# Kept parts of activations, 132 seven-product pairs and shared taps in a two-layer fp32 trunk on one core

## The chip, the core and the metric

The kernel runs on one core of a Trainium2 chip. A core has a matrix engine (TensorE, PE in the profile; its weight loads are PEld), three engines for elementwise work (VectorE or DVE, ScalarE or ACT, GpSimd or POOL) and a queue engine (SyncE, SP) that issues DMA transfers between DRAM and the core's memory. Matmul results land in eight banks of 128 x 512 fp32, called PSUM; everything else lives in SBUF. The metric is the device time of one execution in microseconds, the median of three runs: 2468.08 us before the change (2467.96 to 2468.14).

## What is computed

Two layers over 256 frames of width 2048, all in fp32, batch 1. The first layer's mixer is a gMLP (u and v halves of 6144 each), the second's is latent attention (MLA). Behind each mixer stands a gated MLP with a causal convolution of width 3 over its up projection (2 x 5504 columns).

```python
def gmlp_mixer(x, w_in, ln_g, ln_b, w_s, b_s, w_out):
    z = jax.nn.gelu(x @ w_in)
    u, v = jnp.split(z, 2, axis=-1)
    v = layer_norm(v, ln_g, ln_b)
    ...
    s = jnp.einsum('gij,bnjgd->bnigd', w, v) + jnp.transpose(b_s)[None, None, :, :, None]
    return (u * s.reshape(B, S, GM_HALF)) @ w_out

def conv_ffn(x, w_up, conv_w, conv_b, w_down):
    h = x @ w_up
    h = lax.conv_general_dilated(h, conv_w[:, None, :], window_strides=(1,), padding=[(CONV_W - 1, 0)], ...) + conv_b
    a, g = jnp.split(h, 2, axis=-1)
    return (jax.nn.silu(g) * a) @ w_down

for i in range(DEPTH):        # DEPTH = 2: gMLP, then MLA
    x = layer_norm(ALPHA * x + mixer(x), ...)
    x = layer_norm(ALPHA * x + conv_ffn(x, ...), ...)
```

## The kernel before

**Products.** An fp32 product is built from three passes: each operand is split into a high part (the value rounded to the type fp32r, written by ScalarE) and a low part (the rest, written by VectorE), and TensorE computes high x high, high x low and low x high. The unit of work is a *step*: one weight tile of 128 x 2048, that is two slices k of the contraction by 1024 columns. SP loads it as `raw`, ScalarE casts it to `wh`, VectorE subtracts to `wl`. TensorE then runs 24 matmuls of 128 x 512 for the step (2 k, 2 halves of the frames, 2 halves of the columns, 3 passes).

**Seven-product pairs.** Some steps (116 in the kernel before) treat the pair of k and the halves as a 2 x 2 block product with seven products in place of eight, so 21 matmuls. They need sums of weight blocks, made by VectorE in `raw` in place (`raw<-raw`, one of 1024 columns and two of 512; `sum1`, `sum2`, lines 183 to 192), their high parts `th` on ScalarE and their low parts `tl` on VectorE (two each of 1024 columns; `high`, `rest`, lines 194 to 204). Only 1536 columns of `wh` and `wl` are then needed. They also need sums of activation blocks: `xs` for the projections from x, made once, and `wos`, `dn0s`, `dn1s` for the back projections, made when needed (`blocks`, line 740, and `sums1`, line 766: four instructions on 128 x 128, a cast and a low part on 512).

**Stages.** Steps are numbered over the whole program, and tiles carry the number (`raw184`, `wl126`): v half of the gMLP (0 to 47), u half (48 to 95), its back projection wo (96 to 143), the first up projection (144 to 233), the first down projection dn0 (234 to 277), the MLA, the second up projection, the second down projection dn1. v, u and up go in groups of eight steps that produce 1024 columns; `GROUP_V`, `GROUP_U` and `GROUP_UP` (lines 555 to 557) say which steps of a group are seven-product pairs and where they stand. Before, the ten groups of an up projection have 2, 2, 3, 2, 3, 2, 3, 2, 3, 2 of them.

**Back projections.** wo, dn0 and dn1 are run by the class `Down` (line 917) in two passes over the contraction, the first for 1024 columns and the second, in reverse order, for the other 1024. `SEVEN_WO` and `SEVEN_DN` (lines 558 and 559) list the k of the seven-product pairs of each pass. Before, each quad of four k is split into high and low parts (`woa0_4`, `dn0a0_3`, 128 x 2048: `split4`, line 719) in the first pass and, but for the last four pairs, again in the second (`woa1_4` and so on). The source of the split is the gated activation, which was parked in DRAM (`wosrc4`, `dn0src3`) and is fetched again for each pass (`pb4`, `ab0_3`).

**The convolution.** A group of an up projection is transposed into PSUM (`ht`), and for each tile of 128 columns x 256 frames ScalarE writes y = bias + w2 x, and VectorE adds the two shifted taps with one scalar_tensor_tensor each, of 255 and 254 columns (`taps`, line 1379). Four tiles (two of the a half, two of the g half) make a y of 128 x 4 x 256, from which silu and the gate follow.

**The order of the work.** The class `Plan` (line 292) keeps a list of jobs with an engine, an estimated cost, a due time and needs of buffers, simulates the engines' times and emits the jobs of each engine in the order it finds. `_due` (line 368) sets when the parts of a step are due ahead of its start, `_start` (line 418) when a job could begin, `_fits` whether its buffers are free. The buffers are 22 tiles of 128 x 2048 (`BIG`), `MID` = 3 and `T2` = 5 smaller ones, and the PSUM banks. Engines run their own list in order; DMA issues of SP go out in SP's order, and a DMA that waits holds back those behind it.

Of the kernel before, what the change touches and what calls it, by code (L numbers as in the profile page):

```python
# [563 lines left out]
def trunk(ctx: ExitStack, tc: tile.TileContext, x, xT, gm_in, gm_wout, ffn_up, ffn_dn,  # L564
# [352 lines left out]
    class Down:  # L917

        def __init__(self, n_k, gates, sevens, tag):
# [11 lines left out]
        def give(self, i, tile, after, again, view, stays=None):

            if stays is not None:
                self.here[0, i] = self.here[1, i] = stays, ()
                return
# [440 lines left out]
    def ffn(layer, ln, acc, end, last):  # L1376
        act = [None] * 6

        def taps(tiles, name):
# [33 lines left out]
        def tapped(tiles, name, t, bank, after=(), more=0):  # L1413

            a, m = tiles[0][0], len(tiles) // 2
            scale, add, silu, gate = taps(tiles, name)
            made = []
            for i in range(2 * m):
                due = plan.wide - 0.4 - 0.7 * (2 * m - 1 - i + 4 * more) if bank else t + 6 + i
                j = plan.job("A", maps(256), lambda i=i: scale(i), after if i == 0 else (j,), ready=t, due=due - 1.2,  # L1420
                             need={} if i else {"mid": 1})
                made.append(plan.job("V", adds(255, 2), lambda i=i: add(i), (j, *made[-1:]), ready=t, due=due,
                                     give={} if i < 2 * m - 1 else {"bank": 2} if bank else {"t2": 2}))
# [560 lines left out]
```

## Time and profile before

| | before |
|---|---|
| median of 3 runs | 2468.08 us (2467.96 to 2468.14) |
| the profiled execution, its own time | 2466.72 us |
| its span | 2464.9 us |
| mean granted TensorE clock | 0.998 |
| TensorE's weight loads (PEld) busy | 2053.0 us, 83% |
| DMA moved | 550.33 MB, mean 223 GB/s |
| of it read from / written to DRAM | 518.99 MB / 29.36 MB |
| instructions in the span | 30098 |

The span is the time from the first to the last instruction that the profile shows; the execution's own time is 1.8 us longer. Busy time of an engine is the sum of its instructions' times; the *chain that ended last* is found by going back from the last instruction, at each step to what released it. `PE wo L75 x24` in a timeline is 24 matmuls into tiles named wo, one after another; L75 is the line of a helper through which all instructions go, so that tiles tell more than lines. A group row of VectorE reads: output tile, input tiles, shape out<-in, count | busy us, mean ns of one | idle us ahead of them and what ended that idle time.

### The profile page before, as it was taken

The page shows a single profiled execution, that of the slowest core. Times are in us where ns is not written, and L with a number is a line of the kernel's source. Part 1 is how long each engine was busy: PE and PEld are TensorE (multiplying, and loading weights), DVE is VectorE, ACT ScalarE, POOL GpSimd, SP SyncE. Part 2 cuts the span into 40 slices and gives each one's busy share as a digit, 9 for nine tenths or more (in the row PEclk, how much of TensorE's full clock was granted, in tenths as well). Part 3 has the DMA queues.
Part 4 walks back from the last instruction along what each step waited for, and adds up shares of the span by engine and source line. Part 5 has one row for each costly group of instructions (what it writes and reads, how often), then busy time and mean ns, then how long its engine had stood idle before and what let it go on. Part 6 is the DMA issues. An engine that isn't in the chain of part 4 may idle for free.

```text
span 2464.9 us, 30098 instructions
## 1 busy us (share of the span) xinstructions
PE 2449.7 (99%) x11585; PEld 2053.0 (83%) x11585; DVE 2218.2 (90%) x2459; ACT 1375.1 (56%) x1388; POOL 1.9 (0%) x11
## 2 busy tenths in 40 slices
PE   9999999999999999999999999999999999999998
PEld 7888888888888888888888888988888888888886
DVE  7999899999998899999999897757799999999897
ACT  6555656656554555555566554555465555566562
POOL 0000000000000000000000000000000000000000
PEclk9999999999999999999999999999999999999999
DMA  8566666666676555646567775435556556477774
GB/s 341 207 231 223 217 217 226 239 239 242 236 256 255 206 187 202 232 163 242 202 252 265 267 259 213 169 137 214 185 201 221 187 207 232 163 248 260 272 247 166
DMA packets 127583, 550.33 MB, mean 223 GB/s; under 512 B 14160, under 2 KB 14544, under 8 KB 105808
## 3 DMA queue, kind: packets, MB, share of 16 engines
q1 hardware_dynamic: 126432, 541.99, 61.4%
q10 hardware_dynamic: 1008, 6.42, 0.6%
q8 instruction: 91, 1.49, 0.2%
q14 instruction: 52, 0.43, 0.0%
HBM read 518.99 MB, written 29.36 MB: 222 GB/s over the span
## 4 chain that ended last, share of the span: by engine, by line
PE 99%; DVE 1%; DMA 0%; issue 0%; ACT 0%; DVEq 0%
PE up L75 29%; PE dn L75 15%; PE wo L75 9%; PE v L75 9%; PE u L75 8%; PE up_p L75 5%; PE mo L75 4%; PE dn_p L75 2%; PE u_p L75 2%; PE upf L75 2%; PE v_p L75 2%; PE wo_p L75 1%; PE ht L75 1%; PE mkv L75 1%; PE kn L75 1%; PE qn L75 1%
## 5 line engine op out<-in xcount | busy, mean ns | idle before, releaser
L75 DVE TENSOR_TENSOR wl<-raw,wh 128x2048 fp32r<-128x2048 f32 (+3 forms) x456 | 935.3, 2077 | 51.6 <-ACT wh L75 42.1
L75 ACT CAST wh<-raw 128x2048 fp32r<-128x2048 f32 (+3 forms) x456 | 788.1, 1742 | 260.0 <-DMA raw<-in_ffn_up_dram 86.3
L75 PE MATMUL up<-wh,xhl 128*128 128x512 f32 x1888 | 522.1, 391 | 0.0
L75 ACT CAST th<-raw 128x1024 fp32r<-128x1024 f32 x232 | 244.1, 1053 | 378.8 <-DVE raw L75 376.9
L75 PEld LDWEIGHTS up<-wh,xhl 128*128 128x128 f32 x1888 | 353.2, 188 | 72.0
L75 DVE TENSOR_TENSOR raw<-raw 128x1024 f32<-128x1024 f32 x348 | 302.0, 868 | 9.0
L75 PE MATMUL up<-wl,xhl 128*128 128x512 f32 x944 | 295.0, 390 | 0.0
L75 DVE TENSOR_TENSOR tl<-raw,th 128x1024 fp32r<-128x1024 f32 x232 | 281.3, 1220 | 0.2 <-ACT th L75 0.2
L75 PEld LDWEIGHTS up<-wl,xhl 128*128 128x128 f32 x944 | 177.3, 188 | 36.9
L75 PE MATMUL wo<-wh,woa 128*128 128x512 f32 x586 | 162.8, 390 | 0.0
L75 DVE SCALAR_TENSOR_TENSOR y<-ht,cst,y 128x255 f32<-128x255 f32 x320 | 147.5, 479 | 13.0 <-ACT y L75 7.2
L75 PE MATMUL v<-wh,xhl 128*128 128x512 f32 x558 | 154.0, 391 | 1.6 <-ACT wh L75 1.6
L75 PE MATMUL dn<-wh,dn0a 128*128 128x512 f32 x534 | 147.9, 390 | 0.0
L75 PE MATMUL dn<-wh,dn1a 128*128 128x512 f32 x534 | 147.6, 390 | 0.0
L75 PE MATMUL u<-wh,xhl 128*128 128x512 f32 x516 | 145.2, 391 | 0.0
L75 ACT ACTIVATE y<-ht,cst 128x256 f32<-128x256 f32 x160 | 78.0, 574 | 94.7 <-PE ht L75 94.7
L75 PEld LDWEIGHTS wo<-wh,woa 128*128 128x128 f32 x586 | 109.9, 188 | 22.6
L75 PEld LDWEIGHTS v<-wh,xhl 128*128 128x128 f32 x558 | 104.8, 188 | 24.7 <-ACT wh L75 2.8
L75 PEld LDWEIGHTS dn<-wh,dn1a 128*128 128x128 f32 x534 | 100.2, 188 | 20.8
L75 PEld LDWEIGHTS dn<-wh,dn0a 128*128 128x128 f32 x534 | 100.2, 188 | 20.7
L75 PEld LDWEIGHTS u<-wh,xhl 128*128 128x128 f32 x516 | 96.2, 188 | 19.4
L75 PE MATMUL up_p<-th,xs 128*128 128x512 f32 x288 | 96.6, 389 | 0.0
(503 smaller groups left out, 3734.7 us busy)
## 6 DMA issues: line engine op xcount, KB each, us to landing
raw<-in_ffn_up_dram SPq DMA_DIRECT2D x320, 512.0 KB, 5.0
raw<-in_ffn_dn_dram SPq DMA_DIRECT2D x172, 512.0 KB, 5.8
raw<-in_gm_in_dram SPq DMA_DIRECT2D x99, 512.0 KB, 4.9
raw<-in_gm_wout_dram SPq DMA_DIRECT2D x96, 512.0 KB, 5.3
raw<-in_gm_in_dram SPq DMA_DIRECT2D x46, 1024.0 KB, 6.1
raw<-in_ml_out_dram SPq DMA_DIRECT2D x16, 1024.0 KB, 5.0
raw<-in_ml_b_dram SPq DMA_DIRECT2D x14, 1024.0 KB, 5.8
raw<-in_ffn_up_dram SPq DMA_DIRECT2D x12, 1024.0 KB, 4.8
```

Source lines behind the costliest of these rows:

```text
L75: r = f(*args, **kw)
```

## The change

Four things change together.

1. Seven-product pairs: 132 in place of 116. One more in v, three more in wo's second pass, two more in the second pass of each dn, four more in each up (now 2, 3, 3, 3, 3, 3, 3, 3, 3, 2). Their places in the groups and lists change as well.
2. Back projections: in the first pass, those split quads that the second pass needs again (ten for wo, nine for each dn), and the activation sums of the k that are seven-product pairs in both passes (five each), are written to DRAM by SP (`keep_copy`). The second pass fetches these instead of fetching the source and splitting it again. Sums that only the second pass needs are made from the fetched parts: one more addition of 512 columns (high + low) stands ahead of the four block instructions.
3. The taps: ScalarE writes, beside y, a second map e = w1 x of each tile. VectorE adds the tap of shift 2 per tile as before (254 columns), and the tap of shift 1 for four tiles in one addition of 4 x 255 columns.
4. Planner: `MID` 4 and `T2` 4; a cost function `fused` for scalar_tensor_tensor; and `_start` no longer counts the ends of what a load waits for (the load that precedes it).

```diff
-MID = 3
-T2 = 5
+MID = 4
+T2 = 4
...
+def fused(n, k=1):
+    return k * (0.125 + 0.00106 * n)
...
     def _start(self, j):
-        t = max([self.now[j.eng], j.ready] + [a.end for a in j.after])
+        t = max([self.now[j.eng], j.ready] + [a.end for a in j.after if j.kind != "load"])
...
+    def keep_copy(self, src, dst, lo, due, cost):
+
+        return self.job("S", cost, lambda: self.feed.sq.dma_start(dst, src), (lo,), due=due)
...
-SEVEN_WO = ((8, 14, 20, 26, 30, 34, 40), (40, 34, 28, 22, 16, 12))
-SEVEN_DN = ((8, 14, 18, 22, 26, 32), (34, 28, 22, 16, 12))
+SEVEN_WO = ((14, 20, 24, 26, 30, 34, 40), (42, 40, 38, 34, 30, 26, 22, 20, 12))
+SEVEN_DN = ((8, 14, 18, 22, 26, 32), (36, 32, 28, 26, 22, 18, 14))
...
     def sums1(src8, k, name, after, due, done):
...
+        half = done is None
+        if half:
+            x = tp.tile([P, 2, S], F32, tag="t2", name=f"{name}x", bufs=T2)
 
         def first():
+            if half:
+                hl = src8[0][:, k % 4 : k % 4 + 2].bitcast(F32)
+                ve.tensor_tensor(x, hl[:, :, 0:S], hl[:, :, S : 2 * S], ALU.add)
+            kk = x if half else src8[:, k % 8 // 2]
             blocks(kk[:, 0, :], kk[:, 1, :], [t[:, i, :] for i in range(4)])
...
         def need(self, k, half, due):
             q = k // 4
+            if q not in self.hl and half == 1:
+                t = slot([P, 4, 512], f"{self.tag}a1_{q}", F32R)
+                src, job = self.copies[q]
+                self.hl[q] = t, plan.fetch(src, t.bitcast(F32), (job,), due)
             if q not in self.hl:
...
+                if q in self.again:
+                    t, lo = self.hl[q]
+                    dst = dram.tile([P, 4, 512], F32, name=f"{self.tag}hl{q}")
+                    self.copies[q] = dst, plan.keep_copy(t.bitcast(F32), dst, lo, due + 4.0, 2.9)
             if k in self.sevens[half] and k not in self.sums:
+                if half == 1 and k in self.twice:
+                    r = tp.tile([P, 2, 512], F32R, tag="mid", name=f"{self.tag}s1_{k}", bufs=MID)
+                    src, job = self.copies["s", k]
+                    self.sums[k] = r, plan.job("S", 1.5, lambda: feed.sq.dma_start(r.bitcast(F32), src), (job,),
+                                               due=due - 7.0, need={"mid": 1})
+                    return
+                if half == 1:
+                    self.sums[k] = sums1(self.hl[q], k, f"{self.tag}s1_{k}", {self.hl[q][1]}, due, None)
+                    return
...
+                if k in self.twice:
+                    r, lo = self.sums[k]
+                    dst = dram.tile([P, 2, 512], F32, name=f"{self.tag}sum{k}")
+                    self.copies["s", k] = dst, plan.keep_copy(r.bitcast(F32), dst, lo, due + 4.0, 1.5)
...
             y = tp.tile([P, 4, S], F32, tag="mid", name=f"y{name}", bufs=MID)
+            e = tp.tile([P, 4, S], F32, tag="mid", name=f"e{name}", bufs=MID)
...
                 ac.activation(y[:, i], src, AF.Identity, bias=w(F, 3), scale=w(F, 2))
-
-            def add(i):
+                ac.activation(e[:, i], src, AF.Copy, scale=w(F, 1))
+
+            def tap(i):
                 F, src = tiles[i]
-                for d in (1, 2):
-                    ve.scalar_tensor_tensor(y[:, i, d:S], src[:, 0 : S - d], w(F, 2 - d), y[:, i, d:S], ALU.mult, ALU.add)
...
+                ve.scalar_tensor_tensor(y[:, i, 2:S], src[:, 0 : S - 2], w(F, 0), y[:, i, 2:S], ALU.mult, ALU.add)
+
+            def add():
+                ve.tensor_tensor(y[:, 0:n, 1:S], y[:, 0:n, 1:S], e[:, 0:n, 0 : S - 1], ALU.add)
```

The planner then places everything anew. Three places show it. The first is VectorE's list in the fifth group of the first up projection, before the change. There the taps of the fourth group are due (transposed tiles `ht0_3`; `y0_14` and `y0_16` are the convolution's outputs, four tiles each), and `raw184` holds the weights of the fifth group's first seven-product pair.

```order
L75 TENSOR_TENSOR wl184_7448<-raw184_7415,wh184_7447 128x1536
L75 SCALAR_TENSOR_TENSOR y0_14_7464<-ht0_3_0_0_7454,cst_176,y0_14_7464 128x255
L75 SCALAR_TENSOR_TENSOR y0_14_7464<-ht0_3_0_0_7454,cst_176,y0_14_7464 128x254
L75 SCALAR_TENSOR_TENSOR y0_14_7464<-ht0_3_0_0_7454,cst_176,y0_14_7464 128x255
L75 SCALAR_TENSOR_TENSOR y0_14_7464<-ht0_3_0_0_7454,cst_176,y0_14_7464 128x254
L75 TENSOR_TENSOR raw184_7415<-raw184_7415 128x2x512
L75 SCALAR_TENSOR_TENSOR y0_14_7464<-ht0_3_0_1_7455,cst_176,y0_14_7464 128x255
L75 SCALAR_TENSOR_TENSOR y0_14_7464<-ht0_3_0_1_7455,cst_176,y0_14_7464 128x254
L75 SCALAR_TENSOR_TENSOR y0_14_7464<-ht0_3_0_1_7455,cst_176,y0_14_7464 128x255
L75 SCALAR_TENSOR_TENSOR y0_14_7464<-ht0_3_0_1_7455,cst_176,y0_14_7464 128x254
L75 SCALAR_TENSOR_TENSOR y0_16_7478<-ht0_3_1_0_7468,cst_176,y0_16_7478 128x255
L75 SCALAR_TENSOR_TENSOR y0_16_7478<-ht0_3_1_0_7468,cst_176,y0_16_7478 128x254
```

The same place after the change; `e0_14` is ScalarE's second map.

```order
L75 TENSOR_TENSOR wl184_7512<-raw184_7438,wh184_7511 128x1536
L75 SCALAR_TENSOR_TENSOR y0_14_7526<-ht0_3_0_0_7516,cst_176,y0_14_7526 128x254 x2
L75 SCALAR_TENSOR_TENSOR y0_14_7526<-ht0_3_0_1_7517,cst_176,y0_14_7526 128x254
L75 TENSOR_TENSOR raw184_7438<-raw184_7438 128x2x512
L75 SCALAR_TENSOR_TENSOR y0_14_7526<-ht0_3_0_1_7517,cst_176,y0_14_7526 128x254
L75 SCALAR_TENSOR_TENSOR y0_16_7540<-ht0_3_1_0_7530,cst_176,y0_16_7540 128x254
L75 TENSOR_TENSOR y0_14_7526<-y0_14_7526,e0_14_7527 128x4x255
L75 SCALAR_TENSOR_TENSOR y0_16_7540<-ht0_3_1_0_7530,cst_176,y0_16_7540 128x254
L75 TENSOR_TENSOR raw184_7438<-raw184_7438 128x512 x2
L75 SCALAR_TENSOR_TENSOR y0_16_7540<-ht0_3_1_1_7531,cst_176,y0_16_7540 128x254
```

Of each tile, one instruction is left, the four-tile addition of 4 x 255 columns stands behind the last, and ahead of the first weight sum of `raw184` stand three tap instructions where four stood.

The second place is SP's list in the first pass of dn0, before: loads of weights (`raw`), and among them the fetches of the parked sources (`ab0_3`).

```order
L75 DMA raw238_9725<-in_ffn_dn_dram 128x1024 x2
L75 DMA ab0_2_9753<-dn0src2_8132 128x2048
L75 DMA raw239_9766<-in_ffn_dn_dram 128x1024 x2
L75 DMA raw240_9803<-in_ffn_dn_dram 128x1024 x2
L75 DMA raw241_9848<-in_ffn_dn_dram 128x1024 x2
L75 DMA raw242_9877<-in_ffn_dn_dram 128x1024 x2
L75 DMA ab0_3_9910<-dn0src3_8798 128x2048
L75 DMA raw243_9926<-in_ffn_dn_dram 128x1024 x2
L75 DMA raw244_9960<-in_ffn_dn_dram 128x1024 x2
L75 DMA raw245_9999<-in_ffn_dn_dram 128x1024 x2
L75 DMA raw246_10036<-in_ffn_dn_dram 128x1024 x2
L75 DMA ab0_4_10064<-dn0src4_9472 128x2048
```

The same stretch after; `dn0hl3` is the DRAM copy of the split quad `dn0a0_3`, `dn0sum14` that of the sums of k = 14.

```order
L75 DMA raw239_9879<-in_ffn_dn_dram 128x1024 x2
L75 DMA dn0hl3_9783<-dn0a0_3_9782 128x2048
L75 DMA raw240_9920<-in_ffn_dn_dram 128x1024 x2
L75 DMA dn0sum14_9828<-dn0s0_14_9827 128x1024
L75 DMA raw241_9963<-in_ffn_dn_dram 128x1024 x2
L75 DMA dn0hl4_9874<-dn0a0_4_9873 128x2048
L75 DMA raw242_10001<-in_ffn_dn_dram 128x1024 x2
L75 DMA ab0_3_10030<-dn0src3_8889 128x2048
L75 DMA dn0sum18_9909<-dn0s0_18_9908 128x1024
L75 DMA raw243_10074<-in_ffn_dn_dram 128x1024 x2
L75 DMA dn0hl5_9953<-dn0a0_5_9952 128x2048
L75 DMA raw244_10118<-in_ffn_dn_dram 128x1024 x2
```

Between two loads there now stands a write of 1 MB or half a MB, which waits for the low part of its split or sum, and the loads behind it wait in turn.

The third place is VectorE's list at the start of wo's second pass, before: `woa1_8` and `woa1_9` are quads split again, `wos1_34t` the block sums of k = 34.

```order
L75 TENSOR_TENSOR woa1_9_5011<-pb4_5010,woa1_9_5011 128x4x256
L75 TENSOR_TENSOR wl124_5017<-raw124_4982,wh124_5016 128x2048
L75 SCALAR_TENSOR_TENSOR wos1_34t_5091<-pb4_5010 128x128
L75 TENSOR_TENSOR wos1_34t_5091<-pb4_5010 128x128
L75 SCALAR_TENSOR_TENSOR wos1_34t_5091<-wos1_34t_5091,pb4_5010 128x128
L75 TENSOR_TENSOR wos1_34t_5091<-pb4_5010,wos1_34t_5091 128x128
L75 BN_STATS lnst0_0_3977<-res0_0_4727 128x6 x2
L75 BN_STATS lnst0_1_3978<-res0_1_4729 128x6 x2
L75 TENSOR_TENSOR wl125_5059<-raw125_5020,wh125_5058 128x2048
L75 TENSOR_TENSOR wl126_5099<-raw126_5061,wh126_5098 128x1536
L75 TENSOR_TENSOR raw126_5061<-raw126_5061 128x2x512
L75 TENSOR_TENSOR woa1_8_5090<-pb4_5010,woa1_8_5090 128x4x256
```

And after, from the same step's `wl124` on:

```order
L75 TENSOR_TENSOR wl124_5096<-raw124_4978,wh124_5095 128x1536
L75 TENSOR_TENSOR tl123_5107<-raw123_4947,th123_5106 128x2x512
L75 TENSOR_TENSOR raw124_4978<-raw124_4978 128x2x512
L75 TENSOR_TENSOR raw124_4978<-raw124_4978 128x512 x2
L75 TENSOR_TENSOR tl124_5179<-raw124_4978,th124_5178 128x2x512
L75 TENSOR_TENSOR wos1_38_5059<-wos1_38t_5058,wos1_38_5059 128x512
L75 TENSOR_TENSOR tl124_5179<-raw124_4978,th124_5178 128x2x512
L75 TENSOR_TENSOR wl125_5099<-raw125_5061,wh125_5098 128x2048
L75 TENSOR_TENSOR wl126_5151<-raw126_5102,wh126_5150 128x1536
L75 BN_STATS lnst0_0_3989<-res0_0_4756 128x6 x2
L75 BN_STATS lnst0_1_3990<-res0_1_4758 128x6 x2
L75 TENSOR_TENSOR raw126_5102<-raw126_5102 128x2x512
```

The splits `woa1` are gone from the list, `wl124` has 1536 columns because step 124 is now a seven-product pair, and its sums and low parts have taken the splits' place.

More of the change, by code (lines that the diff above doesn't have):

```diff
@@ L766, in sums1 @@
     def sums1(src8, k, name, after, due, done):
-        kk = src8[:, k % 8 // 2]
         t = tp.tile([P, 4, P], F32, tag="t2", name=f"{name}t", bufs=T2)
@@ L772, in sums1 @@
         flat = t.rearrange("p i t -> p (i t)")
+        half = done is None
+        if half:
+            x = tp.tile([P, 2, S], F32, tag="t2", name=f"{name}x", bufs=T2)
         def first():
+            if half:
+                hl = src8[0][:, k % 4 : k % 4 + 2].bitcast(F32)
+                ve.tensor_tensor(x, hl[:, :, 0:S], hl[:, :, S : 2 * S], ALU.add)
+            kk = x if half else src8[:, k % 8 // 2]
             blocks(kk[:, 0, :], kk[:, 1, :], [t[:, i, :] for i in range(4)])
-            done(one.end)
-        one = plan.job("V", adds(P, 4), first, after, due=due - 7, need={"t2": 1})
+            if not half:
+                done(one.end)
+        one = plan.job("V", adds(P, 4) + half * adds(512), first, after, due=due - 7, need={"t2": 1 + half},
+                       give={"t2": 1} if half else {})
         hi = plan.job("A", copies(512), lambda: ac.copy(r[:, 0], flat), (one,), due=due - 4, need={"mid": 1})
@@ L923, in __init__ @@
             kept = {k // 4 for k in back_order(n_k, 0)[-KEEP:]}
+            self.again = [q for q in self.quads if q not in kept]
+            self.twice = [k for k in sevens[0] if k in sevens[1]]
+            self.copies = {}
             self.left = {}
             for half in range(2):
-                for i in [q // 2 for q in self.quads if half == 0 or q not in kept] + [k // 8 for k in sevens[half]]:
+                for i in [q // 2 for q in self.quads] + [k // 8 for k in sevens[0]] if half == 0 else []:
                     self.left[half, i] = self.left.get((half, i), 0) + 1
-            self.last = (n_k - 1) // 8
             self.parked, self.here = {}, {}
@@ L933, in give @@
             if stays is not None:
-                self.here[0, i] = self.here[1, i] = stays, ()
+                self.here[0, i] = stays, ()
                 return
@@ L948, in f @@
                 self.left[half, i] -= 1
-                if self.left[half, i] == 0 and (half == 1 or i != self.last):
+                if self.left[half, i] == 0:
                     plan.free("big", 1, t)
@@ L1350, in gated @@
                         gate_jobs[8 * D_ + 2 * pr + F].end = j.end
-                j = plan.job("V", adds(256, 2) + adds(512), gated, (shifted[pr // 2],), ready=t, due=t + 4,
+                j = plan.job("V", fused(256, 2) + adds(512), gated, (shifted[pr // 2],), ready=t, due=t + 4,
                              need={"t2": 1}, give={"t2": 1 + pr % 2, "bank": 2, "mid": 3 if last and pr == 3 else 0})
@@ L1382, in taps @@
             y = tp.tile([P, 4, S], F32, tag="mid", name=f"y{name}", bufs=MID)
+            e = tp.tile([P, 4, S], F32, tag="mid", name=f"e{name}", bufs=MID)
+            m = n // 2
+            a = tiles[0][0]
+            s = tp.tile([P, 2, S], F32, tag="t2", name=f"s{name}", bufs=T2)
             w = lambda F, i: cst[:, C_CONV + (layer * 2 * NF_FF + F) * 4 + i :][:, 0:1]
@@ L1402, in gate @@
                 ve.tensor_tensor(act[a // 8][:, a % 8 // 2, 0:m, :], s[:, 0:m], y[:, 0:m], ALU.mult)
-            return scale, add, silu, gate
+            return scale, tap, add, silu, gate
         gate_jobs = [Job("V", 0.0, None) for _ in range(NF_FF)]
@@ L1415, in tapped @@
             a, m = tiles[0][0], len(tiles) // 2
-            scale, add, silu, gate = taps(tiles, name)
+            scale, tap, add, silu, gate = taps(tiles, name)
             made = []
             for i in range(2 * m):
[L1419 to L1422, printed above, removed]
+                due = plan.wide - 0.4 - 1.0 * (2 * m - 1 - i + 4 * more) if bank else t + 6 + i
+                j = plan.job("A", maps(256) + copies(256) + 0.12, lambda i=i: scale(i), after if i == 0 else (j,), ready=t, due=due - 1.2,
+                             need={} if i else {"mid": 2})
+                made.append(plan.job("V", fused(254), lambda i=i: tap(i), (j, *made[-1:]), ready=t, due=due,
                                      give={} if i < 2 * m - 1 else {"bank": 2} if bank else {"t2": 2}))
-            j = made[-1:]
+            j = (plan.job("V", adds(512 * m), add, made[-1:], due=t + 14, give={"mid": 1}),)
             j = (plan.job("A", maps(256 * m), silu, j, due=t + 18, need={"t2": 1}),)
```

9 lines of the change are left out of this document (3 added, 6 removed).

## The prediction

> **What bounds the kernel now.** I read the totals of the page first, then the chain that ended last, then TensorE's own waits, then the busy time by stage.
>
> ```profile
> span 2464.9 us, 30098 instructions
> PE 2449.7 (99%) x11585; PEld 2053.0 (83%) x11585; DVE 2218.2 (90%) x2459; ACT 1375.1 (56%) x1388; POOL 1.9 (0%) x11
> PE 99%; DVE 1%; DMA 0%; issue 0%; ACT 0%; DVEq 0%
> ...
> PE v L75 <- ACT wh L75: 1.6, 1, 1.6
> PE warm L75 <- POOL idle L646: 1.3, 1, 1.3
> PE lnt L75 <- DVE res L75: 1.0, 1, 1.0
> ```
>
> TensorE is busy for all but 15 us of the span, the chain that ended last is 99% TensorE, and the list of all its waits is those three. A kernel like this gets shorter only by giving TensorE fewer matmuls, as long as nobody is late for it. Who could be late is shown by the stages. In order they are: the u half of the gMLP input; the gMLP back projection (wo); the first up projection; the first down projection (dn0); the second up; the second down (dn1) with the tail.
>
> ```profile
> core 0: us, PE busy (x) PEld busy (x) DVE busy (x) ACT busy (x) POOL busy (x), PEclk, DMA share, GB/s
> ...
> 262.00:536.00 274.00, 274.00 (x1332) 230.94 (x1331) 254.31 (x269) 164.69 (x173) 0.00 (x0) 1.00 0.63 221
> 536.00:790.00 254.00, 254.00 (x1148) 211.21 (x1147) 236.09 (x246) 143.28 (x119) 0.00 (x0) 1.00 0.69 248
> 790.00:1268.00 478.00, 478.00 (x2224) 398.99 (x2223) 450.38 (x501) 267.58 (x265) 0.00 (x0) 1.00 0.60 211
> 1268.00:1493.00 225.00, 223.98 (x991) 185.36 (x990) 208.38 (x215) 126.18 (x107) 0.00 (x0) 1.00 0.70 253
> 1750.00:2220.00 470.00, 470.00 (x2174) 391.88 (x2173) 443.49 (x486) 261.33 (x255) 0.00 (x0) 1.00 0.59 209
> 2220.00:2465.00 245.00, 233.78 (x1048) 193.91 (x1046) 218.22 (x243) 126.63 (x113) 0.00 (x0) 0.98 0.69 235
> ```
>
> VectorE (DVE) is the second limit: 92 to 94% busy in every stage that the change touches. ScalarE (ACT) is under 61%. The DMA share is 0.59 to 0.70, higher in the back projections than in the up stages. So a term of the sum is a gain only if VectorE, and in the back projections the DMA queue, can follow.
>
> **What it removes from TensorE.** One plain step is 24 matmuls in 5.44 us:
>
> ```profile
> 535.72 5.44 PE wo L75 x24
> ```
>
> That is 0.227 us each, at a granted clock of 1.00. A seven-product pair takes 21 instead of 24. The order of TensorE has 11464 rows before and 11416 now, with nothing else changed in kind: 16 more pairs x 3 = 48 matmuls, 48 x 0.227 = **10.9 us less**. One of these pairs is in v, 3 in wo, 2 in each dn, 4 in each up.
>
> **What it costs VectorE.**
>
> ```profile
> L75 ACT CAST wh<-raw 128x2048 fp32r<-128x2048 f32 x307 | 583.4, 1910 | 187.3 <-DMA raw<-in_ffn_up_dram 74.9 <-DMA raw<-in_ffn_dn_dram 30.8 <-DMA raw<-in_gm_in_dram 28.9
> L75 ACT CAST th<-raw 128x1024 fp32r<-128x1024 f32 x232 | 244.1, 1053 | 378.8 <-DVE raw L75 376.9 <-PE up L75 1.6
> L75 ACT CAST wh<-raw 128x1536 fp32r<-128x1536 f32 x116 | 171.7, 1480 | 67.6 <-DMA raw<-in_gm_in_dram 18.2 <-DMA raw<-in_ffn_up_dram 11.4 <-DMA raw<-in_ffn_dn_dram 9.5
> L75 DVE TENSOR_TENSOR wl<-raw,wh 128x2048 fp32r<-128x2048 f32 x307 | 695.6, 2285 | 39.8 <-ACT wh L75 33.1 <-DMA raw<-in_ffn_up_dram 2.2 <-PE dn_p L75 2.0
> L75 DVE TENSOR_TENSOR tl<-raw,th 128x1024 fp32r<-128x1024 f32 x232 | 281.3, 1220 | 0.2 <-ACT th L75 0.2
> L75 DVE TENSOR_TENSOR wl<-raw,wh 128x1536 fp32r<-128x1536 f32 x116 | 203.1, 1751 | 6.9 <-ACT wh L75 4.3 <-issue 1.4 <-PE u L75 1.2
> L75 DVE TENSOR_TENSOR raw<-raw 128x512 f32<-128x512 f32 x232 | 160.2, 691 | 6.6
> L75 DVE TENSOR_TENSOR raw<-raw 128x1024 f32<-128x1024 f32 x116 | 141.8, 1222 | 2.4
> L75 DVE SCALAR_TENSOR_TENSOR y<-ht,cst,y 128x255 f32<-128x255 f32 x160 | 76.2, 476 | 7.4 <-ACT y L75 7.2
> L75 DVE TENSOR_TENSOR woa<-pb,woa 128x1024 fp32r<-128x1024 f32 x20 | 24.4, 1219 | 2.0 <-ACT woa L75 2.0
> L75 DVE TENSOR_TENSOR sb<-sb,bsb 128x256 f32<-128x256 f32 x24 | 9.0, 418 | 0.0
> L75 ACT ACTIVATE y<-ht,cst 128x256 f32<-128x256 f32 x160 | 78.0, 574 | 94.7 <-PE ht L75 94.7
> 659.38 0.29 DVE L75 SCALAR_TENSOR_TENSOR wos_40t<-v 128x128 f32<-128x128 f32 x1
> ```
>
> - A further pair: 1.22 + 2 x 0.69 + 2 x 1.22 for the weight sums and their low parts, less 2.285 - 1.751 on wl: +4.51 us. Sixteen: +72 us.
> - Taps: of each of the 172 tiles one 255-wide instruction goes (172 x 0.476 = 81.9). 42 adds of 4 x 255 columns and two of 2 x 255 come. The trace has no such add; between one of 1024 (1.22) and four of 256 (1.68). I take 1.22, since the 1024-wide rows with a broken pattern (tl, woa) also take 1.22: 42 x 1.22 + 2 x 0.69 = 52.6. Net -29 us; at the other end -10.
> - Second pass of the back projections: 10 + 9 + 9 splits of 1.22 go: -34 us.
> - Sums of the activations: 35 before, 27 now. Each is four of 0.29 and one of 0.69 = 1.85, and 8 of the 27 start with one more add of 0.69: -9 us.
>
> The sum is 72 - 29 - 34 - 9 = 0. VectorE's total stays, and work moves: per up layer +18.0 - 14.6 = +3.4 us, v +4.5, wo about 0, each dn -6.2. ScalarE gets 172 more passes over 256 columns (0.574 each, 99 us at most), 28 casts of 1.05 less, and for each further pair two of th less 1.91 - 1.48 on wh, 1.7: about +90 us, 60% busy. It hides behind its own idle time.
>
> **The up stage, closer.** Before, groups with two such pairs and groups with three alternate; now all ten groups but the first and the last have three. Two groups of before:
>
> ```profile
> 1036.30:1123.50 87.20, 87.20 (x403) 72.71 (x402) 82.46 (x92) 49.36 (x49) 0.00 (x0) 1.00 0.58 205
> ...
> L75 DVE TENSOR_TENSOR h<-h,up_p 128x512 f32<-128x512 f32 x4 | 2.7, 686 | 3.6 <-ACT h L75 3.5
> ...
> 1114.73 4.49 DVE L75 TENSOR_TENSOR wl<-raw,wh 128x2048 fp32r<-128x2048 f32 x2
> ...
> 1118.47 0.62 PE L75 MATMUL up<-wl,xhl 128*128 128x512 f32 x2
> ```
>
> VectorE idles 4.7 of 87.2 us, and 3.6 of that in one wait for the end of the pairs, where it is early. That wait is its only reserve. The last two rows show how thin the lead is: the first of the two wl was done at about 1117.0 (half of the 4.49 us), and TensorE read it at 1118.5. Now two groups take TensorE 87.2 - 0.7 = 86.5 us and VectorE 82.5 + 4.5 - 16 x 0.476 + 4 x 1.22 = 84.3: 2.2 us are left, 1.1 for each group. The bubbles that are not that wait were 4.7 - 3.6 = 1.1 for two groups. So it fits, with 0.5 us of reserve in a group of 43. I cost it at 0.5 us of TensorE's waiting for each layer, between 0 and, at the other end of the taps' price (2 x 0.46 more in a group), 0.4 x 9 = 3.6.
>
> **The second pass of wo, closer.** Of the steps 122 to 133 (counted as in the names of the tiles) 8 are now such pairs, where 4 were. There VectorE needs more than TensorE gives, so the lead at the start decides:
>
> ```profile
> 643.44 4.49 DVE L75 TENSOR_TENSOR wl<-raw,wh 128x2048 fp32r<-128x2048 f32 x2
> 650.00 2.66 DVE L75 TENSOR_TENSOR woe<-woe,wo_p 128x512 f32<-128x512 f32 x3 [2.07 <-PE wo_p L75]
> ```
>
> After the last pair of the first pass (step 116) VectorE had waited 2.07 us, with the three next steps ready: a lead of 3 x 5.44 = 16.3 us. The first pass keeps seven pairs and seven sums, so this start stays. From there to the low part that step 126 reads, VectorE's list is: gather and its adds 5.0; four wl of 1751 (steps 122, 123, 124, 126), 7.0, and four of 2285 (120, 121, 125, 127), 9.1; four pairs' sums and low parts, 4 x 5.04 = 20.2; two sums with the further add, 5.1; joins and statistics of the residual, 8 x 0.68 = 5.5: 52. Two neighbours overlap by 0.08 (4.49 for two of 2.285) unless one needs the other, some 53 instructions: 47.8 to 52.0. TensorE gets there after 6 x 5.44 + 3 x 4.76 + 15 x 0.227 = 50.3. So it waits 0 to 1.7 us; I take 0.8. The steps behind regain.
>
> **The DMA queue.** The added writes and reads (28 x 1.05 MB and 15 x 0.52 MB each way, less 15 x 1.05 MB of reading) are issued by SP, in the row of the weight loads.
>
> ```profile
> 1110.00:1120.00 10.00, 10.00 (x46) 8.29 (x45) 9.93 (x10) 7.69 (x6) 0.00 (x0) 1.00 1.01 403
> 536.00:667.00 131.00, 131.00 (x604) 109.32 (x603) 125.07 (x137) 76.78 (x66) 0.00 (x0) 1.00 0.69 252
> 2227.00:2340.00 113.00, 113.00 (x500) 93.63 (x499) 105.57 (x114) 67.78 (x60) 0.00 (x0) 1.00 0.75 257
> ...
> raw<-in_ffn_dn_dram SPq DMA_DIRECT2D x172, 512.0 KB, 5.8
> dn1src<-act SPq DMA_DIRECT2D x5, 1024.0 KB, 4.8
> ```
>
> The first pass of dn1 moved 257 x 113 = 29.0 MB; with nine splits and five sums it is 41.0 MB in 111.6 us, 368 GB/s. Wo's goes from 33.0 to 46.1 MB in 131 us, 352 GB/s. A full stretch moved 403 GB/s, and then both fit. Scaled from share 0.75 to 1, dn1's own mix gives 343 GB/s: 119.7 us, 8 too many. I take the measured full stretch, with 0.35 us of waiting for each dn and 0 for wo. The Trainium skill ("DMA: Bandwidth & Descriptors", section on where 436 GB/s comes from) says that about 358 GB/s a core binds transfers between HBM and SBUF, and 425 was measured with one core streaming. By 358 each dn would wait 114.5 - 111.6 = 2.9 us and the sum would be 5 us higher. The 403 here speaks against it on one core. A write also waits on SP for its split, and loads stand behind it: the closest has VectorE work of 11 us between the split and its own use, against 2.6 (1.05 MB at 403 GB/s) + 5.8 for the load behind it + 1.9 for its cast (the wh row above) = 10.3. Covered, barely.
>
> **Sum.** 2466.72 (the profiled execution: its span of 2464.9 and 1.8 around it) - 10.9 + 2 x 0.5 + 0.8 + 2 x 0.35 = 2458.3. The median shown is 1.36 above that execution: **2459.7 us**, -8.4.
>
> **Rivals.**
> - *VectorE becomes the bound in the up stages.* For it: 97% busy there, leads of 1.5 us, more ScalarE passes ahead of each tap. Against it: the 3.6 us wait shrinks first. If the idle time of before (2.35 a group) were all needed, 1.25 a group would be missing, 22 us in 18 groups; at half of that, 11, the gain is used up: without any waiting the time would be 2468.08 - 10.9 = 2457.2, and with this 2468, within 0.2%.
> - *Slower: the DMA queue is the bound in the first passes of dn.* If 343 GB/s is all that this mix gets, loads fall 8 us behind in each dn, and TensorE with them once VectorE's lead is used up; the same scaling for wo (365 GB/s, 126 us of 131) is full, so any wait of SP there adds some. 2457.2 + 16 = 2473.2 or more. It decides from about 368 GB/s down. Against it: a lead of several steps absorbs part, and 403 was seen.
> - *Better*: nobody waits, and v's wait of 1.6 us goes: 2455.6.
>
> **How the numbers follow.** 0.2% (4.9 us) is about what a measurement of this kernel can tell from no change. The forecast (waits of 0 to 6 us, 2456 to 2463) 0.66; VectorE bound 0.15 and DMA late by 5 to 15 us 0.06, both within 0.2%; DMA bound, slower, 0.10; better 0.03. Faster 0.69, same 0.21, slower 0.10. The range, 2455.5 to 2470, leaves out the slower case and a quarter of the two within 0.2%.
>
> **What would show it.** Right: TensorE busy near 2438.8; its list of waits a few us long; VectorE busy within 15 us of 2218; the new four-tile add near 1.22 us; the second pass without splits on ACT and DVE; DMA share near 0.95 in the first passes. Wrong: TensorE waiting for wl or tl in the up groups (VectorE), or for the up_p banks through the taps; ScalarE's wh waiting for in_ffn_dn loads, more than the 6 us that a load takes, with TensorE's wait behind it (DMA).

## The result: 2454.88 us, 13.1 us less, and below the forecast range

| | before | after |
|---|---|---|
| median of 4 runs | 2468.02 us (2467.96 to 2468.14) | 2454.88 us (2453.82 to 2455.47) |
| ratio, with its 95% interval | | 0.9948 (0.9936 to 0.9960) |
| the profiled execution | 2466.72 us | 2455.47 us |

Faster, as forecast, but by 13.1 us where 8.4 had been forecast, and 0.6 us below the range's low end of 2455.5. The totals of the changed kernel's profile, and the whole list of TensorE's waits (us in total, times, longest):

```profile
span 2453.6 us, 30230 instructions
PE 2439.9 (99%) x11537; PEld 2044.2 (83%) x11537; DVE 2217.4 (90%) x2351; ACT 1431.0 (58%) x1556; POOL 1.9 (0%) x11
...
PE v L75 <- ACT wh L75: 1.6, 1, 1.6
PE warm L75 <- POOL idle L654: 1.3, 1, 1.3
```

No wait has come. One has gone: the third row of before, `PE lnt <- DVE res`, 1.0 us. VectorE's total stands where the forecast put it, 2217.4 against 2218.2 us. Its groups (count | busy, mean ns | idle before) and four stages of it (us, then busy PE, PEld, DVE, ACT, POOL, granted clock, DMA share, GB/s):

```profile
L75 DVE TENSOR_TENSOR tl<-raw,th 128x1024 fp32r<-128x1024 f32 x264 | 319.0, 1219 | 10.7 <-ACT th L75 9.6 <-PE v L75 0.9
L75 DVE SCALAR_TENSOR_TENSOR y<-ht,cst,y 128x254 f32<-128x254 f32 x160 | 72.1, 476 | 14.7 <-ACT e L75 14.7
L75 DVE TENSOR_TENSOR y<-y,e 128x1020 f32<-128x1020 f32 x42 | 50.7, 1214 | 0.3
...
667.40:775.50 108.10, 108.10 (x478) 89.54 (x477) 101.18 (x96) 56.64 (x43) 0.00 (x0) 1.00 0.88 339
1033.50:1120.00 86.50, 86.50 (x399) 72.11 (x398) 84.72 (x85) 56.50 (x67) 0.00 (x0) 1.00 0.55 196
1285.20:1394.70 109.50, 109.50 (x485) 90.68 (x484) 101.78 (x103) 58.99 (x49) 0.00 (x0) 1.00 0.92 346
1394.70:1492.50 97.80, 97.80 (x438) 81.00 (x437) 85.45 (x78) 46.40 (x34) 0.00 (x0) 1.00 0.84 316
```

The four-tile addition takes 1.214 us (1.22 had been taken, between 1.22 and 1.68). Two up groups take 86.5 us of TensorE and 84.7 of VectorE (86.5 and 84.3 forecast). ScalarE's total rose by 56 us, where about 90 had been worked out. The first pass of dn0 moves 346 GB/s and TensorE is busy without a break; 368 had been worked out from 41.0 MB in 111.6 us, and 37.9 MB in 109.5 us were moved.

Step by step, the two traces show where the time went. The time from the first matmul of one step to the first of a later one was taken in both; per matmul more or less, 0.2268 us (5.443 / 24) was set off. What is left is added waiting: all that TensorE lost, whether it stood idle or ran at a lower clock. In 38 of 40 stretches of the program it is within 0.03 us of nothing. Only these places differ:

| place | added waiting, after against before, us |
|---|---|
| steps 0 to 7, the start | +1.36 |
| the end of dn0 and the norm behind it (steps 267 to 274) | -1.25 |
| behind TensorE's last matmul, to the end of the span | -0.5 |
| matmuls: 48 x 0.2268 | -10.9 |
| sum, against 2455.47 - 2466.72 = -11.25 measured | -11.3 |

The start is a matter of the single execution: this profile has a long one, that of before a short one (below). The other two are of the change.

**The end of dn0.** VectorE's timeline, first of before, then of the changed kernel (start, us, operation, [idle before <- releaser]):

```profile
1481.95 0.69 DVE L75 TENSOR_TENSOR res<-res,dn 128x512 f32<-128x512 f32 x1 [3.51 <-PE dn L75]
1482.67 0.69 DVE L75 BATCH_NORM_STATS2 lnst<-res 128x6 f32<-128x512 f32 x1
1483.28 4.48 DVE L75 TENSOR_TENSOR wl<-raw,wh 128x2048 fp32r<-128x2048 f32 x2
1487.68 0.68 DVE L75 TENSOR_TENSOR res<-res,dn 128x512 f32<-128x512 f32 x1
1488.39 0.69 DVE L75 BATCH_NORM_STATS2 lnst<-res 128x6 f32<-128x512 f32 x1
```

```profile
1472.21 2.29 DVE L75 TENSOR_TENSOR wl<-raw,wh 128x2048 fp32r<-128x2048 f32 x1 [0.27 <-ACT wh L75]
1476.48 0.69 DVE L75 TENSOR_TENSOR res<-res,dn 128x512 f32<-128x512 f32 x1 [1.97 <-PE dn L75]
1477.20 0.70 DVE L75 BATCH_NORM_STATS2 lnst<-res 128x6 f32<-128x512 f32 x1
1478.69 2.29 DVE L75 TENSOR_TENSOR wl<-raw,wh 128x2048 fp32r<-128x2048 f32 x1 [0.80 <-ACT wh L75]
1480.90 0.68 DVE L75 TENSOR_TENSOR res<-res,dn 128x512 f32<-128x512 f32 x1
1481.62 0.69 DVE L75 BATCH_NORM_STATS2 lnst<-res 128x6 f32<-128x512 f32 x1
```

Before, two wl (of steps 275 and 276) stand between the first and the second join of the residual; now only one, the other was done ahead of the first join. The second join starts 5.7 us after the first in the kernel before, and 4.4 us after it now, so the norm that TensorE's transposes `lnt` wait for ends sooner.

**The last norm.** The next fence has, for each of the two kernels (before first), the first join of the last norm on VectorE and the last matmul of TensorE:

```profile
2445.21 0.69 DVE L75 TENSOR_TENSOR res<-res,dn 128x512 f32<-128x512 f32 x1 [10.65 <-PE dn L75]
2453.39 0.39 PE L75 MATMUL dn<-wh,dn1a 128*128 128x512 f32 x1
...
2431.67 0.69 DVE L75 TENSOR_TENSOR res<-res,dn 128x512 f32<-128x512 f32 x1 [9.89 <-PE dn L75]
2442.58 0.39 PE L75 MATMUL dn<-wh,dn1a 128*128 128x512 f32 x1
```

The join starts 8.6 us before TensorE's end, and now 11.3. The matmuls of the last steps come in another order, and the first quarter of the output is now complete some twelve matmuls (2.7 us) sooner.

### The profile page after: what moved, and what is told of

Read it like the earlier page. It is cut to its first block, busy times and chain, and to the rows that moved or that the text cites. A ratio compares the mean times of both kernels' runs of the same rounds, so it can differ in the third digit from the quotient of the medians.

```text
span 2453.6 us, 30230 instructions
## 1 busy us (share of the span) xinstructions
PE 2439.9 (99%) x11537; PEld 2044.2 (83%) x11537; DVE 2217.4 (90%) x2351; ACT 1431.0 (58%) x1556; POOL 1.9 (0%) x11
## 4 chain that ended last, share of the span: by engine, by line
PE 99%; DVE 1%; DMA 0%; issue 0%; ACT 0%; DVEq 0%
PE up L75 28%; PE dn L75 15%; PE v L75 8%; PE wo L75 8%; PE u L75 8%; PE up_p L75 6%; PE mo L75 4%; PE dn_p L75 3%; PE u_p L75 2%; PE upf L75 2%; PE v_p L75 2%; PE wo_p L75 2%; PE ht L75 1%; PE mkv L75 1%; PE kn L75 1%; PE qn L75 1%
## 5 line engine op out<-in xcount | busy, mean ns | idle before, releaser
L75 PE MATMUL up<-wh,xhl 128*128 128x512 f32 x1776 | 494.0, 390 | 0.0
L75 ACT CAST th<-raw 128x1024 fp32r<-128x1024 f32 x264 | 278.8, 1062 | 268.0 <-DVE raw L75 245.0
L75 PEld LDWEIGHTS up<-wh,xhl 128*128 128x128 f32 x1776 | 331.9, 188 | 67.9
L75 DVE TENSOR_TENSOR raw<-raw 128x512 f32<-128x512 f32 (+1 forms) x396 | 343.7, 868 | 10.4
L75 DVE TENSOR_TENSOR tl<-raw,th 128x1024 fp32r<-128x1024 f32 x264 | 319.0, 1219 | 10.7 <-ACT th L75 9.6
L75 PE MATMUL up<-wl,xhl 128*128 128x512 f32 x888 | 278.2, 389 | 0.0
L75 PEld LDWEIGHTS up<-wl,xhl 128*128 128x128 f32 x888 | 166.7, 188 | 34.8
L75 ACT ACTIVATE y<-ht,cst 128x256 f32<-128x256 f32 x160 | 96.2, 601 | 109.9 <-PE ht L75 100.8
L75 PE MATMUL up_p<-th,xs 128*128 128x512 f32 x336 | 112.6, 389 | 0.0
L75 PE MATMUL wo<-wl,woa 128*128 128x512 f32 x272 | 87.0, 389 | 0.0
```

The source lines that it names most:

```text
L75: r = f(*args, **kw)
```

## Experiments

Each run is compared with runs of the kernel before on the same chip; "added waiting" is worked out as above, from the one profiled execution of each run. The differences of the medians:

| run | this, us | less before, us | ratio (95%) | added waiting of TensorE, beside the start |
|---|---|---|---|---|
| nosevens | 2466.81 | -0.9 | 0.9997 (0.9989 to 1.0006) | end of dn0 -1.23, tail -0.15, v +0.6 |
| b_start | 2466.08 | -1.6 | 0.9994 (0.9985 to 1.0003) | end of dn0 -1.23, tail -0.6, v +0.6 |
| a_nostart | 2478.68 | +11.0 | 1.0043 (1.0031 to 1.0056) | wo 2nd pass and end 5.6, up 1.6 each, dn 1st pass 3.0 and 4.0, end of dn0 +3.8, tail +4.5 |
| onlysevens | 2490.55 | +22.9 | 1.0094 (1.0079 to 1.0110) | wo 2nd pass 10.4, up 4.4 and 4.3, dn 2nd pass 7.1 each |
| oldtaps | 2462.21 | -5.1 | 0.9980 (0.9971 to 0.9990) | up 3.7 and 3.6 |
| resplit | 2463.79 | -3.5 | 0.9986 (0.9977 to 0.9996) | wo 2nd pass 10.1, dn none |
| dma_half | 2460.49 | -6.8 | 0.9972 (0.9961 to 0.9983) | wo 2nd pass 5.2, dn none |
| dma_full | 2508.25 | +41.0 | 1.0167 (1.0150 to 1.0184) | wo 20.6, dn 1st pass 17.0 and 16.7 |
| more | 2458.73 | -8.4 | 0.9966 (0.9954 to 0.9978) | u 7.6, end of dn0 -0.4, tail +0.3 |
| more2 | 2454.41 | -12.7 | 0.9949 (0.9936 to 0.9961) | u 1.8, end of dn0 -0.5, tail +0.3 |
| after_again | 2454.93 | -12.2 | 0.9949 (0.9937 to 0.9962) | as the change |
| best | 2452.16 | -15.3 | 0.9939 (0.9926 to 0.9953) | dn1's 2nd pass 1.2, end of dn0 -1.2, tail -0.7 |

Part of this added waiting is a slower clock. Away from the two ends of the span, the clock records have stretches of 3.41 us at 0.50: two in a_nostart (from 694 and 1496 us), one in more (500 us) and five in dma_full. Those of a_nostart and more begin within 1.1 us of the end of waits of 2.5, 3.2 and 2.0 us; one stretch costs some 1.7 us (3.41 x 0.5). A wait of 2.5 us in resplit was not followed by one, so these runs give no threshold.

### Matmuls or relief? nosevens and onlysevens

nosevens is the change with the groups and lists of before, onlysevens the kernel before with nothing but the new ones:

```diff
-SEVEN_WO = ((14, 20, 24, 26, 30, 34, 40), (42, 40, 38, 34, 30, 26, 22, 20, 12))
-SEVEN_DN = ((8, 14, 18, 22, 26, 32), (36, 32, 28, 26, 22, 18, 14))
+SEVEN_WO = ((8, 14, 20, 26, 30, 34, 40), (40, 34, 28, 22, 16, 12))
+SEVEN_DN = ((8, 14, 18, 22, 26, 32), (34, 28, 22, 16, 12))
```

> The change without its new groups and lists: 116 pairs, with copies, new taps and the planner's edits. Theory (only the count of matmuls and the two ends of dn count): 2468.0 - 1.7 = 2466.3 us, with VectorE some 70 us less busy (near 2145) and nothing gained from it. Rival (relief of VectorE is worth time by itself): below 2464.

> The kernel before with only the new groups and lists: 132 pairs, old taps, second passes split again, old planner. Theory (VectorE has no room for them: 82.5 + 4.5 of 86.5 us in two up groups, plus 1.1 of gaps; wo's and dn's second passes 9 to 19 us more of VectorE each): TensorE waits, up some 14 us in all, wo 5, dn 3 or more: about 2479 us, slower than before. Rival (the leads absorb it): 2457.1, with no wait but the one at the boundary.

The totals of nosevens, then the first five of TensorE's waits in onlysevens:

```profile
PE 2451.0 (99%) x11585; PEld 2052.7 (83%) x11585; DVE 2161.0 (88%) x2295; ACT 1416.5 (57%) x1528; POOL 1.9 (0%) x11
...
PE up L75 <- DVE wl L75: 5.2, 4, 1.4
PE dn L75 <- DVE wl L75: 4.6, 6, 1.1
PE wo L75 <- DVE wl L75: 4.4, 5, 1.7
PE dn_p L75 <- DVE tl L75: 3.6, 6, 0.9
PE wo_p L75 <- DVE tl L75: 2.4, 4, 1.1
```

57 us less of VectorE work buys nothing by itself: only the two ends of dn are left, as the theory has it. Of the tail's gain only 0.15 us reaches the end of the span here, though VectorE's last instruction ends 0.6 us sooner after TensorE's last matmul. The 0.6 us in v, which b_start has too and the change has not, go with a wait of 0.3 us for ScalarE (`PE v_p <- ACT rows`). And the pairs alone cost 22.9 us: TensorE waits for VectorE's wl and tl in every stage that got pairs. The direction was as expected, the size not: up less (8.7 for 14), wo and dn more (10.4 for 5, 14 for 3). So the relief is not the gain; it is what lets the gain stand.

### What the one line of the planner does: b_start and a_nostart

b_start adds this to the kernel before; a_nostart takes it from the changed one:

```diff
-        t = max([self.now[j.eng], j.ready] + [a.end for a in j.after])
+        t = max([self.now[j.eng], j.ready] + [a.end for a in j.after if j.kind != "load"])
```

> The kernel before with one line of the change alone: the planner no longer counts the end of what a load waits for. Same number of matmuls as before. Theory (order): at the end of dn0 the wl of step 275 now stands ahead of the first join of the residual, so TensorE's wait of 1.0 us at the boundary goes (-1.25 us with what stands behind it), and TensorE runs the last four units of dn1 one after another, so the last norm starts sooner (-0.5): 2466.3 us. Rival (these 1.7 us came from VectorE's relief in the second passes, not from this line): 2468.0, with the wait of 1.0 us still in TensorE's list.

> The changed kernel without that one line. 132 pairs, copies and taps as in the change. Theory (order): the wait at the end of dn0 returns (+1.25), and TensorE's last four units of dn1 come out interleaved, so that the first is done only about 18 matmuls (4.1 us) before the end in place of 42; VectorE's 8.4 us for the first half of the frames then start late, +4 to +5: about 2460.5 us. Rival (relief): 2454.9, no wait at the boundary.

In b_start `PE lnt <- DVE res` is gone from TensorE's list and the stretch at the end of dn0 is 1.23 us shorter, with 116 pairs and the old second pass: that gain, and the tail's, belong to this line. The interval of the ratio still reaches past 1; it is the trace that shows it. Without the line the changed kernel is 11.0 us slower than before. TensorE's waits there, and the same two rows of the tail:

```profile
PE lnt L75 <- DVE res L75: 4.2, 2, 3.2
PE dn L75 <- DVE wl L75: 3.6, 6, 1.3
PE wo L75 <- DVE wl L75: 2.4, 1, 2.4
PE up L75 <- DVE wl L75: 1.9, 4, 0.5
...
2458.40 0.69 DVE L75 TENSOR_TENSOR res<-res,dn 128x512 f32<-128x512 f32 x1 [12.81 <-PE dn L75]
2461.83 0.39 PE L75 MATMUL dn<-wh,dn1a 128*128 128x512 f32 x1
```

The tail came out as expected (the join 3.8 us before TensorE's end, +4.5 us). The waits in wo, up and the first passes of dn did not: neither theory had them, and they make 16 of the 24 us by which this kernel is slower than the change. (In wo, a wait of 2.4 us and a stretch at half clock behind it are 4.1 of the 5.6 us.) By the code, the planner without the line counts each load from the landing of the one ahead of it and so plans later loads; which of its choices then costs what wasn't tried.

### What each relief covers: oldtaps and resplit

oldtaps is the change with the taps of before, resplit the change without the copies to DRAM (the class `Down` and `sums1` of before):

```diff
-                ve.scalar_tensor_tensor(y[:, i, 2:S], src[:, 0 : S - 2], w(F, 0), y[:, i, 2:S], ALU.mult, ALU.add)
+                for d in (1, 2):
+                    ve.scalar_tensor_tensor(y[:, i, d:S], src[:, 0 : S - d], w(F, 2 - d), y[:, i, d:S], ALU.mult, ALU.add)
```

```diff
-            if q not in self.hl and half == 1:
-                t = slot([P, 4, 512], f"{self.tag}a1_{q}", F32R)
-                src, job = self.copies[q]
-                self.hl[q] = t, plan.fetch(src, t.bitcast(F32), (job,), due)
```

> The change with the taps of before: two additions per tile on VectorE, no second map on ScalarE. Theory (VectorE's room in up is 86.5 - 84.7 = 1.8 us in two groups, the old taps take 16 x 0.476 - 4 x 1.214 = 2.8 more): TensorE waits about 1 us in two groups, 9 to 10 in the two up projections, nothing elsewhere: about 2464.5 us. Rival (the taps' saving isn't needed, VectorE's lists have more room than that): 2455 us.

> The change without the DRAM copies: the second passes fetch the source and split it again, as before; 132 pairs, new taps and planner's edits stay. Theory (VectorE gets 10 x 1.22 and 9 x 1.22 us of splits back and the shared sums, and has 101.2 of 108.1 and 85.5 of 97.8 us to do already): TensorE waits in wo's second pass about 8 us, in each dn about 5: about 2473 us, and nothing in up. Rival (a lead from the first pass covers it): 2455 to 2457 us.

TensorE's waits in oldtaps (the first row) and in resplit (the others):

```profile
PE up L75 <- DVE wl L75: 5.4, 4, 1.4
...
PE wo L75 <- DVE woa L75: 3.0, 2, 2.5
PE wo L75 <- DVE wl L75: 2.2, 3, 1.0
PE wo_p L75 <- DVE tl L75: 2.1, 3, 1.0
```

The taps are worth 7.2 us, all in up and only in the middle groups (steps 188 to 219 and 358 to 389), where by our reading the lead of the earlier groups is used up: forecast 9 to 10. The copies are worth 10 us, all in wo. In dn the second split comes back without a wait: VectorE is busy 95.7 of 97.8 us there, where the change has 85.5, and still keeps up. The copies of dn0 and dn1 cover nothing. `MID`, `T2` and `fused` were not tried apart from the rest, so no run tells what they do.

### How near the DMA limit is: dma_half and dma_full

Each copy is followed by a write of half its size, or written twice, to a place that nobody reads:

```diff
+        def both():
+            self.feed.sq.dma_start(dst, src)
+            for o, i in extra:
+                self.feed.sq.dma_start(o, i)
+
-        return self.job("S", cost, lambda: self.feed.sq.dma_start(dst, src), (lo,), due=due)
+        return self.job("S", cost, both, (lo,), due=due)
```

> The change with every DRAM copy of a split followed by one more write of half its bytes to a place that nobody reads; instructions of the engines unchanged. A first pass of dn then moves 37.7 + 4.7 = 42.4 MB in 109.5 us, 387 GB/s. Theory (the queue moves 403 and more): TensorE waits 0 to 1 us, 2455 us. Rival (this mix gets 343 to 358 GB/s, and the change already stands at that limit): loads fall 9 to 14 us behind in each first pass, 2470 us or more.

> The change with every DRAM copy written twice, the second time to a place that nobody reads. A first pass of dn then asks for 37.9 + 12.1 = 50 MB in 109.5 us, 456 GB/s, wo's for 57.8 MB in 131 us, 441 GB/s, over the 403 to 425 seen. Theory (the limit lies at 403 to 425): the loads fall 8 to 14 us behind in each first pass, of which the leads absorb a part: 2465 to 2485 us, with TensorE waiting for wl and wl for wh behind loads of in_ffn_dn. Rival (the lead and the room of the buffers cover even this): under 2458 us.

The first pass of dn0 in dma_half, then in dma_full:

```profile
1289.90:1399.40 109.50, 109.50 (x484) 90.65 (x483) 102.80 (x106) 60.40 (x51) 0.00 (x0) 1.00 0.98 386
...
1304.10:1430.60 126.50, 115.20 (x484) 92.08 (x484) 105.55 (x109) 63.59 (x54) 0.00 (x0) 0.97 1.00 401
```

At 386 GB/s the pass takes the same 109.5 us; at the full share it moves 401 and takes 17 us more, some 3 of them by two stretches at half clock. So the limit of this mix is 401 GB/s, not the 343 scaled from a share of 0.75. The Trainium skill ("DMA: Bandwidth & Descriptors", section on where 436 GB/s comes from) has 358 GB/s bind such transfers; the 386 without a wait speaks against that for this core, which runs alone. In wo dma_half does cost 5.2 us, in the second pass: VectorE, which had been busy 127.4 us in the first pass, got through 121.5 in the same time, as ScalarE's casts waited 34.1 us for wo's weights there in place of 22.3. What VectorE was behind was missing from the lead with which the second pass starts.

### Is there room for more pairs? more, more2 and best

In best the fifth group of v gets a fourth pair, placed as in the third, and the lists of wo and dn one more each. more has k = 8 in place of 16 in dn, and three groups of u with a fourth pair; more2 has two of these, k = 8, and v as in the change. The lists of best against those of the change:

```diff
-SEVEN_WO = ((14, 20, 24, 26, 30, 34, 40), (42, 40, 38, 34, 30, 26, 22, 20, 12))
-SEVEN_DN = ((8, 14, 18, 22, 26, 32), (36, 32, 28, 26, 22, 18, 14))
+SEVEN_WO = ((14, 20, 24, 26, 30, 34, 40), (42, 40, 38, 34, 30, 26, 22, 20, 14, 12))
+SEVEN_DN = ((8, 14, 18, 22, 26, 32), (36, 32, 28, 26, 22, 18, 16, 14))
```

> The change with seven further pairs, placed where the trace shows VectorE idle: one in v (197 of 215 us busy), three in u (252 of 276), one in the second pass of wo, one (k = 8, whose sums are already kept) in the second pass of each dn (66 of 81 us in dn1). Theory (time is the count of matmuls as long as VectorE keeps its lead): 21 x 0.2268 = 4.8 us less than the change, 2450 us; 1 to 2 us of waits may come back in u, at wo's step 126 or at the end of dn0, where the last pair now stands later. Rival (the change is already at VectorE's limit): the waits take it all, 2455 us or more.

> As the last, but with two further pairs in u and none in v: five further pairs, 15 x 0.2268 = 3.4 us less than the change: 2451.5 us. Rival: 2455 us or more.

> The change itself, beside the last two on the same chip: 2455 us, between 2453.5 and 2456 by the clock that the first 12 us are granted (step 0 to 8 in 44.6 or 45.9 us).

> The change with four further pairs where the runs of five and seven showed that VectorE's lead suffices: one in v's fifth group, one in wo's second pass (k = 14), and in the second pass of each dn k = 16 in place of k = 8, so that the last pair stays at k = 14 and the residual's sums are not later. u as in the change. Theory (a pair is worth 3 x 0.2268 us where the lead is over the 5 to 7 us of VectorE that it costs: 12 to 15 us at k = 16, 8 us in v): no new wait, 12 x 0.2268 = 2.7 us less than the change, 2452.2 us. Rival (VectorE needs the lead later, at the end of dn or v): 2454 us or more, with TensorE waiting for tl, wl or the norm's res there.

TensorE's waits in more (without the start's):

```profile
PE uT L75 <- DVE sg L75: 3.1, 2, 2.0
PE s L75 <- DVE vb L75: 1.0, 3, 0.3
PE lnt L75 <- DVE res L75: 0.6, 1, 0.6
```

The u half was the wrong place. VectorE idles 23 us there, but each group with a fourth pair cost 0.7 to 4.4 us, at the gates `uT` and `s`, for the 0.68 it saved (of the 4.4, some 1.7 are the stretch at half clock behind a wait of 2.0): idle time that sits behind a chain of waits is not room. And with k = 8 the wait for the norm came back in part, as its sums are joined later, and the tail's gain of 0.5 us turned into a loss of 0.3. Without these two, best comes out at the 2452.2 expected. That the number is met so closely is luck: the theory had no new wait, the trace has 1.2 us in dn1's second pass, and five executions lie between 2451.9 and 2454.4. It is 15.3 us under the kernel before, against 12.2 and 13.1 for the change. Its interval and the change's overlap.

## What held of the prediction, and the step that failed

- **Fewer matmuls, 10.9 us: right.** 48 x 0.2268, with none of it given back.
- **VectorE's ledger: right.** Total within 1 us, up groups within 0.4 us, the four-tile addition at the price taken.
- **The waits taken for that ledger, 2.5 us: wrong.** The 0.5 us for each up, 0.8 in wo and 0.35 for each dn were set between 0 and a high end; all measured 0. In wo it was close: with a little less lead (dma_half) 5.2 us came at once. In up the lead is small but nothing is short until about 2.8 us are added in two groups (oldtaps). In dn there was room for the DMA (up to 386 GB/s) and for VectorE (resplit).
- **The failed step: an edit that was not costed at all.** The prediction has no term for the planner's `_start` line and says nothing of the wait `PE lnt <- DVE res`, 1.0 us, that it quotes as the third of TensorE's waits. Its best case gave away v's 1.6 us instead, which stayed, and the result lies below even that case (2455.6). b_start shows that this line takes the wait at the end of dn0 (-1.25) and moves the tail (-0.5). Both can be read off the order of the instructions: the wl of step 275 ahead of the first join, and the last matmuls of dn1. And a_nostart shows that the line carries more than these two ends: without it the changed kernel is 24 us slower and the whole gain is lost.
- **From 2459.7 to 2454.9:** 2.5 of waits that did not come, 1.75 of those two ends, and 0.5 that lies within the spread of the start. Without the waits the sum is 2457.2, inside the range; the 1.75 us take it to 2455.4, just below the range, and the 0.5 on top are luck.
- **The rivals.** VectorE as the bound in up, 2468: half right, it is the state of oldtaps, and the taps' saving is what keeps it away. The DMA as the bound of dn's first passes: not here; it decides from 401 GB/s, not 368.

## What to carry to other kernels

In this kernel a saving on the engine that bounds was worth its full price as long as the feeder kept its lead. Test each relief alone, since some cover much (wo's copies, the taps) and some nothing (dn's copies). When an edit touches a scheduler's rule, compare the order at every stage's end with the list of waits, however short, before costing it at nothing. Idle time of a feeder is room only where its lead, step by step, is longer than what is added.

## What the runs showed of the hardware

Step 0 took 6.25 to 8.49 us in the 14 profiles, whatever the kernel. Runs of one kernel spread by about as much; that the start makes this spread is likely, but one execution of each run was profiled, so it isn't shown. One microsecond of the start before, and four after (the granted clock is the third number from the end):

```profile
8.00:9.00 1.00, 1.00 (x6) 0.83 (x5) 0.73 (x2) 0.76 (x2) 0.00 (x0) 1.00 0.90 328
...
8.00:9.00 1.00, 1.00 (x4) 0.81 (x3) 0.74 (x2) 0.75 (x2) 0.00 (x0) 0.50 0.93 340
9.00:10.00 1.00, 1.00 (x4) 0.81 (x3) 1.00 (x2) 0.41 (x1) 0.00 (x0) 0.50 1.00 406
10.00:11.00 1.00, 1.00 (x4) 0.71 (x3) 0.76 (x2) 0.81 (x2) 0.00 (x0) 0.50 1.15 465
11.00:12.00 1.00, 1.00 (x5) 0.82 (x4) 0.98 (x2) 1.00 (x2) 0.00 (x0) 0.80 1.01 428
```

In the long start the clock is halved for 3.4 us (three microseconds at 0.50 and 0.4 of the fourth), some 4 us after the last of the seven warming matmuls began (3.9 us) and 2 after the first weights were there (6.1). The Trainium skill ("TensorE: Matmul & The Clock Gate", part 1 on the clock gate) tells of a half clock after an idle window of about 3.4 us that runs freely of the kernel's start; the length, and that it comes by chance, agree with that here. An idle window of that length is not in this trace: TensorE stood idle for 1.6 us (4.49 to 6.08), and the profile of before has the same pause without a half clock behind it. So what sets it off isn't shown.

In best and more2 step 0 was longest (8.47 and 8.49 us), though the rows give a clock of 1.00:

```profile
8.00:9.00 1.00, 1.00 (x4) 0.81 (x3) 0.79 (x2) 0.70 (x2) 0.00 (x0) 1.00 0.97 385
```

Four matmuls stand in this microsecond of best, as in the rows at 0.50, against six in that of before. The clock record of these two profiles begins only at 12.1 us, and what has no record counts as 1.00; until about then most of their matmuls come 0.43 us apart, later 0.23. Four further profiles (onlysevens, oldtaps, resplit, dma_half) show the same with records that begin at 9.2 to 10.2 us. Where a record begins late, the spacing of the matmuls tells the clock.
